# A two-layer diffusion step on one core: raw weights of late pairs loaded a pair ahead, ten early pairs, prompts' products a pair later

## The chip, the cores and the metric

The kernel runs on one core of a Trainium2 chip. Its engines are TensorE (PE, the matrix products), VectorE (DVE), ScalarE (ACT), GpSimd (POOL) and SyncE (SP), which only issues transfers; ACT and POOL issue some too. Each works through its own list of instructions in order. The metric is the device time of one execution in microseconds (us), the median of the runs shown.

## The reference

Two layers work on a prompt of 128 tokens and a sample of 1024 tokens, with the same weights. In each layer a normalised and modulated input is multiplied by one wide matrix; its columns feed three branches (a gated convolution, attention and multi-scale pooling) and the gates by which the branches are merged:

```python
    hn = rms_norm(x, g_pre) * (1 + scale) + shift
    proj = hn @ w_in
    (a_b, a_c, a_x, a_z, q_down, kv_down, b_z, c_u, c_z, merge_logits) = jnp.split(proj, split_points, axis=-1)
    y_a = jax.nn.silu(a_z) * (a_b * centred_conv3(a_c * a_x, conv_w, conv_b))
    ...
    y_b = jax.nn.silu(b_z) * attn
    y_c = jax.nn.silu(c_z) * multiscale_pool(c_u, pool_w, pool_scale)
    branches = jnp.einsum('bsnc,ncd->bsnd', jnp.stack([y_a, y_b, y_c], axis=2), w_branch)
    merged = jnp.sum(gates * branches, axis=2)
    out = rms_norm(merged @ w_o, g_post)
    return x + gate * out, own_latent
```

## The kernel before

**Products.** All values are float32. Each operand of a large product is split into a high part (a cast to float32r) and a low part (what is left), and a product is the sum of three matmuls, high by high, low by high and high by low (`mm3`, line 107). The cast is mostly ACT's (`a_copy`, line 68), the subtraction DVE's (`sub`, line 88). A matrix for the sample has its feature index across the partitions and 1024 tokens, in two halves of 512.

**Pairs.** The product with `w_in` is done in 29 pairs of output blocks (class `Pair`), each for the whole sample by a scheme with seven products instead of eight; a product is four `mm3`, so 12 matmuls of 128x512. They have the names 11, 21, T2, T1, T3, 22 and T4 by the part of the input that they use. The prompt's product with the same columns is 24 matmuls of 128x256. The first two products and the prompt's need only half of the input's preparation. So nine pairs (`EARLY`) run twice: as "early" pairs at the start of a layer (11, 21 and the prompt's, in `early`), before the whole input is ready, with the result of 11 stored in `d_p1`; and as "late" pairs at the end (the other five products, in `run`). The other 20 (`ORDER`) are "full" pairs and run between them.

**Preparation.** `Pair.prep` is a generator, whose first step loads the raw weights (1 MB a pair, as two tiles), and whose later steps form sums and differences (POOL, DVE), casts (ACT) and subtractions (DVE). `ahead` pulls the generators of the next pairs one step at a time after each product; so what lies where in each engine's list follows from these pulls. `tick` does the same for background work such as `conv_gen`, `s_pool` (the sample's pooling, line 1068 loads its input), `p_pool` (the prompt's pooling, transposes at line 1108), the modulation's products and, at the start of a layer, the normalisation of the prompt (`hnp_gen`) and of the input's second half (`gB`), which ends in `t_gen`, the sums over the input that the later products use.

**Buffers and queues.** 44 slots of 128x1040 (`S()`, tiles named s) are given out in turn; an operation that writes a new slot waits until the one handed out 44 earlier is no longer read. `put` (lines 125 and 130) has a store issued by SP some steps later. SP issues in order, so a store that waits for its data holds the loads behind it.

**After the pairs.** `mid_phase` starts `p_pool`, runs `merge` for branch 0 and for branch 2 (the second adds to what the first left: a product by the gate on DVE, an addition on POOL and a store issued by POOL, line 984), and `produce` makes the attention's operands. It begins with POOL's memsets of `q32` (line 1301) and of `qa` (line 1313), into which ACT then copies. Weights of these stages are split by `pump`, two of three casts on POOL (`p_copy`, line 82). After attention, `last_merge` and `out_phase` end the layer; the latter's `first` and the generators `gP` (prompt) and `gB` carry the start of the next layer.

Of the kernel before, what the change touches and what calls it, by code (L numbers as in the profile page):

```python
# [26 lines left out]
EARLY = (0, 1, 2, 3, 4, 5, 6, 7, 25)  # L27
# [6 lines left out]
def hybrid_step_kernel(ctx: ExitStack, tc: tile.TileContext, I, O):  # L34
# [32 lines left out]
    def a_copy(out, in_):  # L67
        act.copy(out=out, in_=in_)  # L68
# [128 lines left out]
    lead = [6]  # L197
    freed = [0]
# [371 lines left out]
    class Pair:  # L570
        def __init__(self, l, p, kind):
            self.l, self.p, self.kind = l, p, kind
            self.gen = self.prep()

        def prep(self):
            raw = [S(), S()]
            g, h = SOURCE[self.p]
            for i in range(2):
                if g == 14:
                    sp.dma_start(out=raw[i][:, 0:1024], in_=I["w_in2"][self.l, i])  # L580
                    continue
                for t in range(2):
                    src = I["w_in"][self.l, g, 2 * i + t].rearrange("p (k c)->p k c", k=2)
                    sp.dma_start(out=raw[i][:, 512 * t:512 * t + 512].rearrange("p (k c)->p k c", k=2),
                                 in_=src[:, :, 256 * h:256 * h + 256])
# [31 lines left out]
            if not late_:  # L617
                low(raw[0], w[0])
            if early_:
# [64 lines left out]
    def early(l, units, epis, mid, pend):  # L684

        gP, gB = pend
        for us in [units[0:3]] + [[u] for u in units[3:]]:
            first, steps = len(us) > 1, 2 if us[0] in units[-2:] else 1
            p1 = []
            for u in us:  # L690
                ready(u)
                h = H()
                a_copy(h, u.prod(u.w[0], 0, "11"))
                act.dma_start(out=d_p1[EARLY.index(u.p)], in_=h)
                p1.append(h)
                if mid:
                    next(mid, None)
                ahead(None, 3 - steps, steps)
                if not first or u is us[1]:
                    tick()  # L700
            for u, h in zip(us, p1):
                v = H()
                add(v, u.prod(u.w[1], 0, "21"), h)
                epis[u.p][0](0, 0, v)
                ahead(None, 3 - steps, steps)
                if not first or u is not us[1]:
                    tick()
            finish(gP)
            for u in us:
                epis[u.p][1](u.prompt())  # L710
                ahead(None, 3 - steps, steps)
                tick()
            mid = None
# [135 lines left out]
    ORDER = list(range(8, 16)) + list(range(19, 23)) + [16, 17, 18, 23, 24, 26, 27, 28]  # L849
# [6 lines left out]
    def in_phase(l, e, mid, pend):  # L856
# [8 lines left out]
        ya, yp = [], S(F32R)  # L865
# [29 lines left out]
        return ya, yp  # L895
# [64 lines left out]
    def merge(l, n, y, yp, first, hooks=()):  # L960
# [15 lines left out]
        def out(ps):  # L976
# [11 lines left out]
        for g in range(2):  # L988
# [5 lines left out]
            for m in range(4):  # L994
                out(prod_m(B, m, y_get(y), 0))
# [12 lines left out]
            for m in range(4):  # L1008
                out(prod_m(B, m, y_get(y), 1))
# [245 lines left out]
    def mid_phase(l, ya, ypa):  # L1255
# [4 lines left out]
        yc, ypc = [], S(F32R)  # L1260
        gp = spawn(p_pool(l, ypc))
# [19 lines left out]
    def produce(l, R):  # L1281
# [16 lines left out]
        A["q32"] = q32  # L1298
        for h in range(8):
# [11 lines left out]
        qa = S()  # L1311
        A["qa"] = qa
        pool.memset(qa[:, 0:1024], 0.0)
# [504 lines left out]
    def out_phase(l, mg, pt):  # L1818
# [54 lines left out]
    with tc.manual_schedule():  # L1873
# [21 lines left out]
        next(units[0].gen)  # L1895
        load_mod(1)
        load_mod(3)
        next(units[1].gen)
        next(units[2].gen)
# [23 lines left out]
        def mid():  # L1923
# [6 lines left out]
            hn_first(0, 0, xt[0], (2, 3))  # L1930
            next(gP)
# [16 lines left out]
        for kp in range(4):  # L1948
            for j in range(2):
                x = xt[0][kp][:, 512 * j:512 * j + 512]  # L1950
                mul(x, x, r, eng=dve if kp < 2 else pool)
# [3 lines left out]
        hn_first(0, 0, xt[0], (0, 1))  # L1955
        gP, gB = spawn(hnp_gen(0, xp)), spawn(first_b())
# [3 lines left out]
        for l in range(L):  # L1960
            R = mid_phase(l, *in_phase(l, units, then if l else mid(), pend))
            A = produce(l, R)
            yb = attention(l, R, A)
            finish(gmod)
# [117 lines left out]
```

## Time and profile before

| | before |
|---|---|
| runs | 2825.68, 2824.93, 2816.12 us; median 2824.93 |
| profiled execution | 2818.2 us by its own time, span 2816.4 us |
| PE busy | 2587.5 us (92%) |
| DVE, ACT, POOL busy | 1806.8, 1078.9, 879.0 us |
| moved by DMA | 371.01 MB, mean 132 GB/s |

The span is what the profiler saw between the first and the last instruction; the own time of the execution is a little longer. A busy share is a mean over stages with different limits, so the stages are looked at apart: layer 0 has its early pairs up to about 170 us, full pairs to 600, late pairs to 770, merges to 943, `produce` to about 983 and attention to 1280; layer 1 has its early pairs from 1446 to 1570, late pairs from 1980 to 2168, merges to 2301 and `produce` to about 2340.

### The profile page before, as it was taken

The page shows a single profiled execution, that of the slowest core. Times are in us where ns is not written, and L with a number is a line of the kernel's source. Part 1 is how long each engine was busy: PE and PEld are TensorE (multiplying, and loading weights), DVE is VectorE, ACT ScalarE, POOL GpSimd, SP SyncE. Part 2 cuts the span into 40 slices and gives each one's busy share as a digit, 9 for nine tenths or more (in the row PEclk, how much of TensorE's full clock was granted, in tenths as well). Part 3 has the DMA queues.
Part 4 walks back from the last instruction along what each step waited for, and adds up shares of the span by engine and source line. Part 5 has one row for each costly group of instructions (what it writes and reads, how often), then busy time and mean ns, then how long its engine had stood idle before and what let it go on. Part 6 is the DMA issues. An engine that isn't in the chain of part 4 may idle for free. (4 is left out here: it accounts for less than half of the span.)

```text
span 2816.4 us, 32523 instructions
## 1 busy us (share of the span) xinstructions
PE 2587.5 (92%) x11672; PEld 2051.2 (73%) x11672; DVE 1806.8 (64%) x2434; ACT 1078.9 (38%) x1752; POOL 879.0 (31%) x772
## 2 busy tenths in 40 slices
PE   4899999999899889899977999999988898998997
PEld 2777777777677767677866888888766677776785
DVE  4845555657747578886577444666675657888655
ACT  4532222332322257774345222323322214776621
POOL 2322211102122646754032222111211174566402
PEclk7899999999999999999998999999999999999999
DMA  7333345546497400005254222444447751000433
GB/s 276 110 125 97 97 154 176 189 149 191 159 321 246 153 5 8 23 23 180 90 182 158 84 71 83 154 146 164 164 146 273 252 201 27 5 8 31 124 112 112
DMA packets 213506, 371.01 MB, mean 132 GB/s; under 512 B 20576, under 2 KB 105568, under 8 KB 213344
## 3 DMA queue, kind: packets, MB, share of 16 engines
q1 hardware_dynamic: 170896, 275.32, 30.2%
q10 hardware_dynamic: 31680, 56.38, 5.4%
q0 software_dynamic: 10768, 37.23, 3.5%
q8 instruction: 92, 1.51, 0.2%
q14 instruction: 70, 0.57, 0.1%
HBM read 254.45 MB, written 112.23 MB: 130 GB/s over the span
## 5 line engine op out<-in xcount | busy, mean ns | idle before, releaser
L107 PE MATMUL p<-s,s 128*128 128x512 f32 (+3 forms) x10876 | 2464.8, 386 | 142.1 <-ACT s L68 47.2
L107 PEld LDWEIGHTS p<-s,s 128*128 128x128 f32 (+1 forms) x10876 | 1953.9, 191 | 625.9 <-DVE s L88 55.6
L88 DVE TENSOR_TENSOR s<-s,s 128x1024 fp32r<-128x1024 f32 (+7 forms) x565 | 628.3, 1125 | 317.2 <-ACT s L68 106.9
L68 ACT CAST s<-s 128x1024 fp32r<-128x1024 f32 (+3 forms) x341 | 333.4, 998 | 554.0 <-DVE s L88 319.4
L88 DVE TENSOR_TENSOR h<-p,h 128x512 f32<-128x512 f32 (+1 forms) x480 | 317.0, 661 | 333.8 <-PE p L107 239.2
L88 POOL TENSOR_TENSOR s<-s,s 128x512 f32<-128x512 f32 (+2 forms) x109 | 215.7, 1982 | 857.1 <-DMA s<-in_w_in_dram 625.3
L88 DVE TENSOR_TENSOR s<-h,s 128x512 fp32r<-128x512 f32 (+4 forms) x316 | 302.7, 970 | 129.2 <-ACT s L79 64.8
L79 ACT ACTIVATE h<-p 128x512 f32<-128x512 f32 (+2 forms) x364 | 208.5, 573 | 227.2 <-PE p L107 214.9
L79 ACT ACTIVATE h<-h 128x512 f32<-128x512 f32 (+1 forms) x196 | 123.0, 629 | 315.4 <-DVE h L88 260.9
L88 POOL TENSOR_TENSOR h<-h,h 128x512 f32<-128x512 f32 (+2 forms) x72 | 98.1, 1362 | 302.5 <-DVE h L88 173.7
L79 ACT ACTIVATE s<-p 128x512 fp32r<-128x512 f32 x288 | 174.1, 604 | 2.4 <-POOL h L88 2.4
L88 DVE TENSOR_TENSOR h<-h,h 128x512 f32<-128x512 f32 (+3 forms) x122 | 90.9, 745 | 95.6 <-ACT h L79 93.0
L1536 DVE TENSOR_REDUCE c<-p 128x1 f32<-128x448 f32 x256 | 147.9, 611 | 6.6 <-PE p L107 6.5
L82 POOL TENSOR_SCALAR s<-s 128x1024 fp32r<-128x1024 f32 (+2 forms) x65 | 79.4, 1227 | 208.8 <-DMA s<-in_w_o_dram 64.8
L88 POOL TENSOR_TENSOR s<-s 128x512 f32<-128x512 f32 x94 | 132.3, 1407 | 29.6 <-DVE s L88 27.1
L68 ACT COPY h<-p 128x512 f32<-128x512 f32 (+2 forms) x108 | 51.6, 478 | 217.6 <-PE p L107 207.6
L88 POOL TENSOR_TENSOR s<-h,s 128x512 fp32r<-128x512 f32 x64 | 89.0, 1391 | 126.5 <-ACT s L79 125.1
L68 ACT CAST s<-h 128x512 fp32r<-128x512 f32 (+5 forms) x92 | 47.8, 524 | 164.0 <-DVE h L88 99.0
L68 ACT COPY s<-p 64x512 f32<-64x512 f32 (+3 forms) x116 | 64.2, 566 | 112.1 <-PE p L107 75.2
L88 DVE TENSOR_TENSOR s<-p,s 128x512 f32<-128x512 f32 (+2 forms) x118 | 72.6, 631 | 47.6 <-PE p L107 31.4
L88 POOL TENSOR_TENSOR s<-s,h 128x512 f32<-128x512 f32 x26 | 40.8, 1574 | 116.6 <-DVE h L100 76.1
L107 PE MATMUL p<-s,h 128*128 128x512 f32 (+1 forms) x184 | 57.2, 421 | 15.1 <-ACT s L68 13.2
(122 smaller groups left out, 944.9 us busy)
## 6 DMA issues: line engine op xcount, KB each, us to landing
s<-in_w_in_dram SPq DMA_DIRECT2D x296, 256.0 KB, 4.2
s<-in_w_mod_dram SPq DMA_DIRECT2D x48, 512.0 KB, 4.9
d_gate<-h ACTq DMA_DIRECT2D x96, 256.0 KB, 4.6
s<-d_gate SPq DMA_DIRECT2D x64, 256.0 KB, 5.6
s<-in_w_br_dram SPq DMA_DIRECT2D x24, 512.0 KB, 4.7
s<-in_xT_dram SPq DMA_DIRECT2D x16, 512.0 KB, 6.3
s<-d_ya POOLq DMA_DIRECT2D x16, 512.0 KB, 10.7
s<-d_yc POOLq DMA_DIRECT2D x16, 512.0 KB, 10.6
```

Source lines behind the costliest of these rows:

```text
L68: act.copy(out=out, in_=in_)
L79: act.activation(out=out, in_=in_, func=func, scale=scale, bias=bias)
L82: pool.tensor_scalar(out=out, in0=in_, scalar1=1.0, scalar2=0.0, op0=ALU.mult, op1=ALU.add)
L88: eng.tensor_tensor(out=out, in0=in0, in1=in1, op=op)
L107: pe.matmul(out=out, lhsT=lhsT, rhs=rhs, start=start, stop=stop)
L1536: dve.reduce_max(out=mv[:, i, qt:qt + 1], in_=ps[:, 0:448], axis=AX.X)
```

## The change

- `EARLY` has a tenth pair, 26, which leaves `ORDER`.
- The loads of a pair's raw weights become `load(i)`. An early pair loads its second half only after the cast of the first. In `in_phase` the loads of the next two late pairs are issued before the present pair runs. At the start of layer 0 the first halves of four pairs are loaded between the modulation's weights, the second halves after them.
- `early` takes four pairs (layer 0) or three (layer 1) together: first all their products 11, with only the first half of each pair's weights ready, then all their products 21, then 11 and 21 of the next pair, and only then the prompt's products of all of them.
- `p_pool` is started three pairs before the end of `in_phase` in place of the start of `mid_phase`.
- In `merge`, the additions of the second half of the sample (c = 1) go from POOL to DVE and their stores from POOL to SP. `pump` has ACT do the casts outside of attention. `produce` clears `qa` before `q32`.
- At the boundary of the layers the loads of `gB` start later in layer 0, and `gB` goes ahead of `gP`. At the start the products of the third and fourth input tiles with the row norm, on POOL, come after the first half of the normalisation.

```diff
-EARLY = (0, 1, 2, 3, 4, 5, 6, 7, 25)
+EARLY = (0, 1, 2, 3, 4, 5, 6, 7, 25, 26)
...
-            if i % 3 == 1:
+            if i % 3 == 1 or not att[0]:
                 a_copy(hi[:, 0:n_], st[:, 0:n_])
...
+        def first(self):
+
+            while not self.w0:
+                next(self.gen)
 
         def prep(self):
...
+            self.load(0)
+            if self.kind != "early":
+                self.load(1)
+            raw = self.raw
             yield
...
             if early_:
+                self.load(1)
+                yield
                 w[1] = high(raw[1])
...
+        us = units[:nb]
+        us[0].first()
+        for i, u in enumerate(us):
+            p1(u)
+            if i + 1 < nb:
+                us[i + 1].first()
+            keep1(u)
+            next(mid, None)
+            step()
+        for _ in mid:
+            pass
+        for i, u in enumerate(us):
+            ready(u)
+            if i == 0:
+                ready(us[1])
+            p2(u)
+            ahead(None, 1) if i else None
+            tick()
+        finish(gP)
+        for i, u in enumerate(units[nb:]):
+            steps = 2 if u in units[-2:] else 1
+            ready(u)
+            p1(u)
+            ahead(None, 3 - steps, steps)
+            keep1(u)
+            tick()
+            p2(u)
+            ahead(None, 3 - steps, steps)
+            tick()
+            for x in (us if i == 0 else []) + [u]:
+                epis[x.p][1](x.prompt())
                 ahead(None, 3 - steps, steps)
                 tick()
...
+            if u[min(i + 1, len(u) - 1)].kind == "late":
+                for y in u[i + 1:i + 3]:
+                    y.load(0), y.load(1)
+            if i == len(u) - 3:
+                ypc.append(S(F32R))
+                gp.append(spawn(p_pool(l, ypc[0])))
             run(l, x, epis[x.p], None if last else u[i + 1], hooks)
...
-            if first:
+            if not first:
+                add(x, x, t[:, 512:1024], eng=None if c else pool)
+            if first or c:
                 put(dst, x)
             else:
-                add(x, x, t[:, 512:1024], eng=pool)
                 pool.dma_start(out=dst, in_=x)
...
+        qa = S()
+        A["qa"] = qa
+        pool.memset(qa[:, 0:1024], 0.0)
         for h in range(8):
             z0 = 32 if h % 2 else 96
             pool.memset(q32[h][z0:z0 + 32, 0:1024], 0.0)
...
         finish(gA)
         gB = post_chunk(l, 1, B, True)
-        next(gB)
+        if l + 1 == L:
+            next(gB)
...
-                next(gP), next(gB)
-                yield
-                next(gP), next(gB)
+                next(gB), next(gP)
+                yield
+                next(gB), next(gP)
                 spawn(gB), spawn(gP)
```

The first place is SP's list among layer 1's late pairs, before: `d_p_88` is `d_p1`, in_w_in the raw weights (two tiles a pair), `d_yc` a store of the sample's pooling.

```order
540 L647 DMA h_15912<-d_p_88 128x512
541 L584 DMA s_15928<-in_w_in_dram 128x2x256 x2
542 L584 DMA s_15929<-in_w_in_dram 128x2x256 x2
543 L125 DMA d_yc<-h_15897 128x512
544 L130 DMA d_yc<-h_15964 128x512
545 L1068 DMA s_16025<-d_u 128x2x512
546 L647 DMA h_16045<-d_p_88 128x512
547 L584 DMA s_16061<-in_w_in_dram 128x2x256 x2
548 L584 DMA s_16062<-in_w_in_dram 128x2x256 x2
```

The same place of the same list after the change:

```order
551 L665 DMA h_15817<-d_p_88 128x512
552 L1129 DMA h_15920<-d_z 128x512
553 L1129 DMA h_15922<-d_z 128x512
554 L588 DMA s_15940<-in_w_in_dram 128x2x256 x2
555 L588 DMA s_15943<-in_w_in_dram 128x2x256 x2
556 L665 DMA h_15946<-d_p_88 128x512
557 L130 DMA d_yc<-h_15991 128x512
558 L130 DMA d_yc<-h_16044 128x512
559 L1114 DMA s_16067<-d_u 128x2x512
560 L588 DMA s_16071<-in_w_in_dram 128x2x256 x2
561 L588 DMA s_16074<-in_w_in_dram 128x2x256 x2
562 L665 DMA h_16077<-d_p_88 128x512
```

Before, the load of `d_p1` for the next pair stands ahead of raw weights that are loaded while that pair's predecessor runs; after, the raw weights of a pair stand one load of `d_p1` earlier than the pair that uses them, so those behind the store at 558 belong to a pair later.

The second place is POOL's list where the second merge of layer 0 ends and `produce` begins, before:

```order
184 L88 TENSOR_TENSOR s_6841<-s_6841 128x512
185 L984 DMA d_part<-s_6841 128x512
186 L88 TENSOR_TENSOR s_6860<-s_6860 128x512
187 L984 DMA d_part<-s_6860 128x512
188 L88 TENSOR_TENSOR s_6879<-s_6879 128x512
189 L984 DMA d_part<-s_6879 128x512
190 L88 TENSOR_TENSOR s_6914<-s_6914 128x512
191 L984 DMA d_part<-s_6914 128x512
192 L82 TENSOR_SCALAR s_6973<-s_6965 128x1024
193 L1301 MEMSET s_6981 32x1024
...
200 L1301 MEMSET s_6988 32x1024
201 L1313 MEMSET s_7043 128x1024
```

After, in the same list:

```order
165 L88 TENSOR_TENSOR s_6833<-s_6833 128x512
166 L1030 DMA d_part<-s_6833 128x512
167 L88 TENSOR_TENSOR s_6814<-s_6814 128x512
168 L1052 DMA d_partp<-s_6814 128x512
169 L1346 MEMSET s_7002 128x1024
170 L1349 MEMSET s_6994 32x1024
...
177 L1349 MEMSET s_7001 32x1024
178 L88 TENSOR_TENSOR s_7082<-s_7012,s_6990 128x1024
```

Of the eight equal memsets the first and the last are shown. The four additions with their stores and the cast of a weight have left this list, and `qa` (128x1024) is cleared ahead of the eight tiles of `q32`.

The third place is DVE's list in layer 1's early pairs, before: lines with 128x1024 on s tiles are subtractions that give low parts (`s_11438` and `s_11474`, the second halves of the weights of the second and third pair), `h_11509` and `h_11521` the prompt's normalised rows.

```order
1214 L88 TENSOR_TENSOR h_11455<-p_11456,h_11342 128x512
1215 L88 TENSOR_TENSOR s_11438<-s_11414,s_11437 128x1024
1216 L88 TENSOR_TENSOR h_11476<-p_11477,h_11377 128x512
1217 L88 TENSOR_TENSOR s_11474<-s_11415,s_11473 128x1024
1218 L88 TENSOR_TENSOR h_11500<-s_11440 128x512
1219 L103 TENSOR_SCALAR h_11509<-p_11504,cols_0_101 128x128 x4
1220 L88 TENSOR_TENSOR s_11503<-h_11509,s_11502 128x512
1221 L103 TENSOR_SCALAR h_11521<-p_11516,cols_0_101 128x128 x4
1222 L88 TENSOR_TENSOR s_11503<-h_11521,s_11502 128x512
```

After, in the same list (`s_11458` is the low part of the third pair's second half, and `h_11502` the result of that pair's product 21):

```order
1223 L103 TENSOR_SCALAR h_11482<-p_11477,cols_0_101 128x128 x4
1224 L88 TENSOR_TENSOR s_11476<-h_11482,s_11475 128x512
1225 L103 TENSOR_SCALAR h_11494<-p_11489,cols_0_101 128x128 x4
1226 L88 TENSOR_TENSOR s_11476<-h_11494,s_11475 128x512
1227 L88 TENSOR_TENSOR s_11458<-s_11363,s_11457 128x1024
1228 L88 TENSOR_TENSOR h_11502<-p_11503,h_11397 128x512
1229 L88 TENSOR_TENSOR h_11522<-s_11460 128x512
```

The third pair's low part has moved from ahead of the prompt's rows to behind them.

## Rows read from the trace of the kernel before

**Rows 1.** The page's first part: busy time, share and instructions by engine.

```profile
PE 2587.5 (92%) x11672; PEld 2051.2 (73%) x11672; DVE 1806.8 (64%) x2434; ACT 1078.9 (38%) x1752; POOL 879.0 (31%) x772
```

**Rows 2.** Stretches: length, busy time (instructions) by engine, granted clock, DMA share, GB/s.

```profile
170.00:600.00 430.00, 429.13 (x2048) 336.76 (x2047) 241.24 (x299) 117.73 (x152) 83.35 (x70) 1.00 0.43 140
600.00:770.00 170.00, 154.74 (x665) 117.33 (x664) 115.98 (x169) 52.65 (x77) 27.25 (x22) 0.96 0.53 168
770.00:943.00 173.00, 160.97 (x666) 127.59 (x665) 109.05 (x180) 36.94 (x57) 52.67 (x65) 0.95 0.81 284
943.00:983.00 40.00, 32.08 (x144) 25.14 (x143) 17.09 (x30) 10.06 (x29) 26.11 (x27) 0.91 0.25 73
...
1446.00:1570.00 124.00, 94.11 (x479) 78.76 (x478) 86.22 (x86) 59.02 (x80) 39.84 (x28) 0.86 0.48 161
...
1980.00:2168.00 188.00, 171.81 (x724) 137.27 (x723) 129.89 (x177) 58.94 (x85) 37.83 (x41) 0.95 0.54 179
2168.00:2301.00 133.00, 117.94 (x494) 93.46 (x493) 83.85 (x150) 26.62 (x42) 42.27 (x46) 0.95 0.79 277
2301.00:2340.00 39.00, 33.75 (x148) 25.51 (x147) 19.46 (x33) 10.83 (x32) 24.35 (x25) 0.91 0.24 68
```

**Rows 3.** PE's waits from 600 to 770: releaser, us, times, longest.

```profile
PE p L107 <- DMA s<-in_w_mod_dram: 5.8, 2, 5.0
PE p L107 <- ACT h L68: 4.4, 1, 4.4
```

**Rows 4.** PE's waits from 1980 to 2168.

```profile
PE p L107 <- ACT s L68: 8.6, 2, 8.4
...
PE p L107 <- DVE h L88: 2.5, 1, 2.5
```

**Rows 5.** PE's waits from 805 to 943.

```profile
PE p L107 <- DVE s L100: 4.0, 1, 4.0
...
PE p L1108 <- DMA s<-d_uzp: 2.7, 1, 2.7
PE p L107 <- ACT s L68: 2.3, 1, 2.3
```

**Rows 6.** PE's waits from 2168 to 2301.

```profile
PE p L1108 <- DMA s<-d_uzp: 6.4, 1, 6.4
PE p L107 <- DVE s L100: 5.3, 1, 5.3
PE p L107 <- ACT s L68: 2.5, 1, 2.5
```

**Rows 7.** DVE's timeline in both layers' late pairs; brackets: idle before, releaser.

```profile
727.86 2.49 DVE L88 TENSOR_TENSOR s<-s,s 128x512 f32<-128x512 f32 x2 [10.50 <-DMA s<-in_w_in_dram]
...
2087.10 2.48 DVE L88 TENSOR_TENSOR s<-s,s 128x512 f32<-128x512 f32 x2 [9.95 <-DMA s<-in_w_in_dram]
```

**Rows 8.** SP's waits from 1980 to 2168 (line 130 stores d_yc).

```profile
SPq L130 <- DVE h L88: 15.4, 2, 10.3
```

**Rows 9.** POOL's timeline at the end of layer 0's second merge.

```profile
949.91 1.30 POOL L88 TENSOR_TENSOR s<-s 128x512 f32<-128x512 f32 x1
951.50 0.56 POOL L984 DMA_DIRECT2D d_part<-s  x1 [0.30 <-POOL s L88]
...
953.21 7.86 POOL L1301 MEMSET s<- 32x1024 f32 x8
```

**Rows 10.** ACT's timeline at the start of layer 0's operands.

```profile
962.12 1.93 ACT L68 COPY s<-p 128x128 f32<-128x128 f32 x6 [17.55 <-POOL s L1313]
```

**Rows 11.** DVE's timeline in layer 1's early pairs, subtraction alone and sum beside POOL.

```profile
1495.76 1.22 DVE L88 TENSOR_TENSOR s<-s,s 128x1024 fp32r<-128x1024 f32 x1
...
1508.55 3.42 DVE L88 TENSOR_TENSOR s<-s,s 128x1024 f32<-128x1024 f32 x1 [0.51 <-POOL s L103]
```

**Rows 12.** PE's timeline in layer 1's early pairs.

```profile
1457.83 0.80 PE L107 MATMUL p<-s,s 128*128 128x512 f32 x1 [7.85 <-ACT s L68]
...
1483.79 5.34 PE L107 MATMUL p<-s,s 128*128 128x256 f32 x24 [10.23 <-ACT s L68]
```

More of the change, by code (lines that the diff above doesn't have):

```diff
@@ L197, in hybrid_step_kernel @@
     lead = [6]
+    att = [False]
     freed = [0]
@@ L573, in __init__, with load @@
             self.gen = self.prep()
-        def prep(self):
[L576 to L585, printed above, removed]
+            self.raw = [None, None]
+            self.w0 = False
+        def load(self, i):
+            if self.raw[i] is not None:
+                return
+            self.raw[i] = r = S()
+            g, h = SOURCE[self.p]
+            if g == 14:
+                sp.dma_start(out=r[:, 0:1024], in_=I["w_in2"][self.l, i])
+                return
+            for t in range(2):
+                src = I["w_in"][self.l, g, 2 * i + t].rearrange("p (k c)->p k c", k=2)
+                sp.dma_start(out=r[:, 512 * t:512 * t + 512].rearrange("p (k c)->p k c", k=2),
+                             in_=src[:, :, 256 * h:256 * h + 256])
+        def first(self):
+            while not self.w0:
+                next(self.gen)
+        def prep(self):
+            self.load(0)
+            if self.kind != "early":
+                self.load(1)
+            raw = self.raw
             yield
@@ L686, in early, with p1, keep1, p2 @@
         gP, gB = pend
[L687 to L710, printed above, removed]
+        nb = 4 if l == 0 else 3
+        def p1(u):
+            u.ps1 = u.prod(u.w[0], 0, "11")
+        def keep1(u):
+            u.h1 = H()
+            a_copy(u.h1, u.ps1)
+            act.dma_start(out=d_p1[EARLY.index(u.p)], in_=u.h1)
+        def p2(u):
+            v = H()
+            add(v, u.prod(u.w[1], 0, "21"), u.h1)
+            epis[u.p][0](0, 0, v)
+        us = units[:nb]
[29 more added lines that the diff above has]
+                epis[x.p][1](x.prompt())
                 ahead(None, 3 - steps, steps)
                 tick()
-            mid = None
     def run(l, u, epi, nxt=None, hooks=()):
@@ L847, in hybrid_step_kernel @@
     SOURCE += [(12, 1), (13, 0), (13, 1), (14, 0)]
-    ORDER = list(range(8, 16)) + list(range(19, 23)) + [16, 17, 18, 23, 24, 26, 27, 28]
+    ORDER = list(range(8, 16)) + list(range(19, 23)) + [16, 17, 18, 23, 24, 27, 28]
     def units_of(l):
@@ L864, in in_phase @@
         flush()
-        ya, yp = [], S(F32R)
+        ya, yp, ypc, gp = [], S(F32R), [], []
         def load_ya(m):
@@ L894, in in_phase @@
         finish(g2)
-        return ya, yp
+        return ya, yp, ypc[0], gp[0]
     def conv_gen(l):
@@ L974, in fetch, with out @@
             got.append((t, d_part[4 * g + m, c]))
-        def out(ps):
+        def out(ps, c):
             t, dst = got.popleft()
@@ L994, in merge @@
             for m in range(4):
-                out(prod_m(B, m, y_get(y), 0))
+                out(prod_m(B, m, y_get(y), 0), 0)
                 if hooks:
@@ L1008, in merge @@
             for m in range(4):
-                out(prod_m(B, m, y_get(y), 1))
+                out(prod_m(B, m, y_get(y), 1), 1)
                 if hooks:
@@ L1253, in kvq_post, with mid_phase @@
         return R
-    def mid_phase(l, ya, ypa):
+    def mid_phase(l, ya, ypa, ypc, gp):
         lead[0] = 4
@@ L1259, in mid_phase @@
         R = kvq_post(l)
-        yc, ypc = [], S(F32R)
-        gp = spawn(p_pool(l, ypc))
+        yc = []
         def load_yc(m):
@@ L1894, in hybrid_step_kernel @@
         units = units_of(0)
-        next(units[0].gen)
+        for u in units[:4]:
+            u.load(0)
         load_mod(1)
         load_mod(3)
-        next(units[1].gen)
-        next(units[2].gen)
+        for u in units[:4]:
+            u.load(1)
         xp = S()
@@ L1947, in hybrid_step_kernel, with times_r @@
         r = rstd(bsum(norm_x(0)), DM)
[L1948 to L1951, printed above, removed]
+        def times_r(kps, eng):
+            for kp in kps:
+                for j in range(2):
+                    x = xt[0][kp][:, 512 * j:512 * j + 512]
+                    mul(x, x, r, eng=eng)
+        times_r((0, 1), dve)
         x_new()
@@ L1962, in hybrid_step_kernel @@
             A = produce(l, R)
+            att[0] = True
             yb = attention(l, R, A)
+            att[0] = False
             finish(gmod)
```

5 lines of the change are left out of this document (2 added, 3 removed).

## The prediction

> **What bounds the kernel now.** The page comes first: TensorE (PE) is busy for 2587.5 of 2816.4 us [rows 1], so whatever the other engines save counts only where PE stands still for them. The next view is the table of stretches, which shows where that is. In the full pairs of layer 0 PE is busy 429.13 of 430 us at a granted clock of 1.00; in the late pairs, in the merges, in the first part of the attention's operands and at the start of layer 1 it is idle and its clock falls below 1.00 [rows 2]. The clock has two levels, 1.2 and 2.4 GHz, so a mean of 0.95 over 133 us means that 13.3 us ran at the lower level, which costs up to 133 x 0.05 = 6.65 us on top of the idle time. The third view, PE's waits in a stretch, names what came last before each wait [rows 3 to 6]; the timeline of another engine, or its own waits, then show why that work was late [rows 7 to 12]. The change touches each of those places, and nothing in the attention or in the full pairs, where I take no difference.
>
> **The change part by part.** TensorE's work stays the same: 10 + 19 pairs in place of 9 + 20, and a pair split into early and late still has seven products and one for the prompt. The tenth early pair costs 1 MB of loads, one cast and one subtraction more per layer; all lie in stretches in which DMA's share is about half and ScalarE's (ACT's) busy time 52.65 of 170 us [rows 2], so I cost them at nothing. If that cover were gone, they would cost their own time, some 3 us a layer.
>
> *Raw weights a pair ahead.* In both layers VectorE (DVE) sits idle for about 10 us in the late pairs, waiting for in_w_in [rows 7]. SyncE issues its transfers in order, and a store of d_yc that waits for DVE holds it, once for 10.3 us [rows 8]; the weights stand behind that store. What is then late on DVE is late on ACT and in the end on PE: a wait of 4.4 us in layer 0 [rows 3], of 8.4 and 2.5 us in layer 1 [rows 4]. In the order after, the two loads of the pair after next stand ahead of such a store. I take these waits as gone. The wait of 5.0 us for the modulation weights in layer 0 stays: their load is not moved. Of the clock's cost, 170 x 0.04 = 6.8 and 188 x 0.05 = 9.4 us, I give back 1.6 and 2.1, since other waits lie in the same stretches. That makes -6 in layer 0 (between 0 and -4.4 - 5.8 - 6.8 = -17) and -13 in layer 1 (between 0 and -8.6 - 2.5 - 9.4 = -20.5).
>
> *The prompt's pooling earlier.* Its load of d_uzp, its transposes and its small additions now start three pairs before the end of the late pairs in place of the start of the first merge. PE waits for exactly these three things: d_uzp, ACT's cast ahead of the pool_w product, and DVE's L100 ahead of the second merge's prompt product. That is 2.7 + 2.3 + 4.0 = 9.0 us in layer 0 [rows 5] and 6.4 + 2.5 + 5.3 = 14.2 us in layer 1 [rows 6]. With 3 us of each stretch's clock cost (173 x 0.05 = 8.65 and 133 x 0.05 = 6.65) I get -12 and -17, between 0 and -17.6, and 0 and -20.9. The work itself does not vanish: some 10 us of small DVE operations move into late pairs, where DVE is busy 129.89 of 188 us [rows 2]; PE's eight transposes are in its queue there and can wait for the same load. I charge a quarter of the 23.2 us for that: +6 (between 0 and +23).
>
> *GpSimd relieved.* At the end of the second merge GpSimd (POOL) does an addition (1.30 us) and a DMA issue (0.56 us) per product, one every 2.18 us, and begins the 7.86 us of memsets only at 953.21 [rows 9]. ACT's copies into qa wait for the memset behind these, idle for 17.55 us until 962.12 [rows 10], and PE waits 7.9 us for ACT. After, the last four additions are DVE's and their stores SyncE's (4 x 2.18 = 8.7 us off POOL), the casts of weights are ACT's, and qa's memset stands ahead of the others, which is 7.86 us more. Together 16.6 us, more than the 7.9 us waited, so the wait can go entirely; next late are the products with the cosines, still behind the eight memsets. I take -9 in layer 0 (idle 40 - 32.08 = 7.9 and 40 x 0.09 = 3.6 of clock, so between 0 and -11.5), -5 in layer 1 (39 - 33.75 = 5.25 and 3.5, between 0 and -8.8). The eight additions a layer on DVE last some 0.7 us each and lie beside 109.05 busy of 173 us, so they cost nothing; without that cover they would cost 5.5 us.
>
> *Early pairs.* Layer 1: PE waits 10.23 us for ACT's cast of the prompt's normalised rows [rows 12]. The new order has only five products ahead of that chain where there were six (third unit's second product now needs a subtraction that stands behind the chain in DVE's queue), but the wait for the third unit's cast behind GpSimd's work, 7.85 us [rows 12], mostly goes. One product is 12 x 429.13 / 2048 = 2.5 us by [rows 2]. A further subtraction, for the fifth unit, falls into the sums that DVE and POOL make beside each other, where one of 128x1024 took 3.42 us in place of 1.22 [rows 11]. I take +6, between -8 and +15: two such waits of 5 to 6 us, less half the 7.85. Layer 0: the first normalisation loses POOL's company, but lows of the second to fourth units fall behind the other half of it; I take 0, and for the bounds the longest wait of [rows 12] either way: -10 and +10.
>
> On those sums the Trainium skill has a rule (SBUF — State Buffer, "SBUF: two separate sides"): VectorE with two SBUF inputs and GpSimd take turns at a shared pair of ports, and of the one that comes second it says "the other fully blocks". By it a subtraction of 1.22 us would take as long as the rest of a GpSimd addition and its own time; 3.42 us agrees with that only in kind. It speaks against the new place of GpSimd's products with the row norm at the start, which now run beside DVE's subtractions; by it the start would come out at the end of its range, and the time at 2782 us.
>
> **The sum.** -6 - 13 - 12 - 17 + 6 - 9 - 5 + 6 + 0 = -50 us. The profiled execution took 2818.2 us by its own time (span 2816.4), so 2768; the runs shown have a median of 2824.9, 6.7 us above it, and one lies below it, so I add half of that: **2772 us**.
>
> **The rivals.**
>
> *The raw weights are late all the same.* They only change places in SyncE's queue; a load a pair ahead needs its slot a pair earlier, and in layer 0 the modulation weights and two d_yc stores still stand between two such loads. SyncE was held 15.4 us in two waits by one store line in layer 1 [rows 8]. For it: DMA waits move easily. Against: a late pair has five products, 5 x 2.5 = 12.5 us, more than the 10.5 us that DVE waits. The 19 us are lost and the time is 2772 + 19 = 2791. Chance 0.14.
>
> *The early pairs lose more.* If the third unit's second product, the fourth's first and the fifth's each wait as long as the longest wait there now (10.23 us), less the one that there is, it is 20 us more: 2792. For it speaks that DVE's order puts the subtraction behind the whole chain; against, that PE is idle there already. Chance 0.10.
>
> *GpSimd is not what holds the operands.* The copies into qa find another wait, such as ACT's own casts of weights in front of them, and the 14 us stay: 2786. Chance 0.06.
>
> *Slower: the ring of slots turns against it.* Slots are handed out in turn, 44 of them, and each waits until the one handed out 44 before is free. Raw weights loaded a pair ahead hold two slots a pair longer, and the tenth early pair takes four slots more. If from then on every late pair's preparation waited for a slot, PE would wait in each of 20 late pairs; at the 10 us of [rows 7] at most, at 4 us likely, that is +80 - 50 = +30 against the profile, 2850. It decides from 50 / 20 = 2.5 us per late pair. Against: the pair whose tiles lie 44 back is done when the loads are issued. Chance 0.08.
>
> **How the numbers follow.** The forecast above has a chance of 0.62, with a range of its own from 2750 to 2788. The rivals hold 0.14, 0.10, 0.06 and 0.08. The range that holds 8 in 10 leaves out the slot case and the best sums of all bounds: 2748 to 2808. A measurement of this kernel tells some 0.5% from no change, 14 us: below 2811 counts as faster. The forecast, most of the first two rivals and the third lie there, 0.84; half of the slot case and what is left of the others lie within, 0.09; the rest is slower, 0.07.
>
> **What the profile after would show.** DVE's two idle times for in_w_in in the late pairs are gone, and so are PE's waits for d_uzp and for L100 in the merges; the transposes for it lie in the late pairs. ACT's wait for the memset of qa is short, and POOL's busy time is lower by the 16 additions of 1.30 us (21 us) and by the casts. The stretch from 1446 has one wait of 10 us ahead of the third unit's second product. The clock of the merges is 0.98 or more. I am wrong if the late pairs still show waits for in_w_in, if PE waits for the slots' loads in several late pairs, or if the two starts of layers together take over 20 us more than now.

## The result and the profile after

The changed kernel takes 2779.57 us (median of 4 runs, 2774.80 to 2783.02), the kernel before beside it 2820.84 us. The ratio is 0.9852 (95% interval 0.9825 to 0.9880), 1.5% faster: 41 us, where 50 against the profile and 53 against the first median were forecast, with 2772 us and a range from 2748 to 2808.

The page after, first lines (busy time, share, instructions; the granted clock in 40 slices):

```profile
span 2773.0 us, 32545 instructions
...
PE 2569.7 (93%) x11672; PEld 2037.3 (73%) x11672; DVE 1812.7 (65%) x2452; ACT 1103.0 (40%) x1779; POOL 820.1 (30%) x715
...
PEclk8799999999999999999987999999999999999999
```

TensorE (PE) has as many instructions as in [rows 1], GpSimd (POOL) 57 fewer and 59 us less to do, ScalarE (ACT) 24 us more. The table of stretches after, cut at nearly the same places of the program as [rows 2], with one difference: layer 0's late pairs end, and its merges begin, at 805 here. In the trace before that place is 810, so 40 us of [rows 2]'s stretch from 770 to 943 are still late pairs.

```profile
185.00:615.00 430.00, 429.12 (x2049) 336.82 (x2048) 241.35 (x300) 117.59 (x152) 81.84 (x70) 1.00 0.43 140
615.00:805.00 190.00, 182.64 (x795) 141.50 (x794) 139.25 (x209) 62.40 (x92) 36.36 (x42) 0.98 0.65 216
805.00:930.00 125.00, 118.54 (x511) 94.01 (x510) 89.09 (x145) 32.17 (x49) 35.72 (x37) 0.99 0.85 300
930.00:960.00 30.00, 29.96 (x139) 23.22 (x137) 17.32 (x32) 11.89 (x34) 12.21 (x13) 1.00 0.27 72
1421.00:1571.00 150.00, 108.92 (x525) 88.04 (x524) 91.83 (x89) 62.78 (x85) 39.38 (x28) 0.84 0.44 148
...
1980.00:2151.00 171.00, 160.91 (x685) 129.04 (x684) 128.32 (x189) 59.28 (x86) 34.59 (x40) 0.97 0.57 191
2151.00:2270.00 119.00, 111.84 (x478) 88.36 (x477) 86.03 (x143) 28.62 (x41) 29.62 (x30) 0.99 0.84 295
2270.00:2306.00 36.00, 36.00 (x170) 28.48 (x168) 19.17 (x35) 15.22 (x40) 18.21 (x19) 1.00 0.39 124
```

The trace before, cut there too:

```profile
600.00:810.00 210.00, 194.74 (x838) 149.84 (x837) 140.09 (x197) 63.01 (x91) 40.85 (x44) 0.97 0.58 191
810.00:943.00 133.00, 120.97 (x493) 95.08 (x492) 84.94 (x151) 26.58 (x42) 39.07 (x44) 0.94 0.80 283
```

The merges' clock rises from 0.94 and 0.95 to 0.99, and `produce` has no idle time left on PE in its first 30 us. The start of layer 1 went the other way: 150 - 108.92 = 41 us idle and a clock of 0.84, where [rows 2] had 30 us and 0.86.

To split the 42 us by stage I read when the same matmul (by its number on PE) starts in each trace, and take the differences. The tenth early pair moves 24 matmuls of 128x512 and 24 of 128x256 a layer from the end to the start; I count them as 8.4 us (the kernel with that pair alone is 8.2 and 8.8 us longer there). Worked out from PE's records, us, after minus before:

```
stage                              difference   without the move   forecast
start and early pairs, layer 0        +14.2           +5.8             0
late pairs, layer 0                   -23.2          -14.8            -3
merges and operands, layer 0          -18.6          -18.6           -21
boundary and early pairs, layer 1     +26.1          +17.7            +6
late pairs, layer 1                   -20.0          -11.6           -10
merges and operands, layer 1          -17.6          -17.6           -22
full pairs, attention, the rest        -2.9           -2.9             0
sum                                   -42.0          -42.0           -50
```

(The forecast's +6 for the pooling's work in the late pairs is split between the two. Of the -2.9 in the parts for which nothing was forecast, about -6 lies in layer 1's attention and +3 in the others; the last section shows how much such a part varies.) PE's waits in the merges of layer 1, after (releaser, us in total, times, longest):

```profile
PE p L107 <- DVE s L88: 5.1, 3, 3.5
PE p L107 <- DMA s<-d_ya: 1.9, 1, 1.9
```

Of the three waits of [rows 6], 14.2 us, none is left. In the boundary the picture is another; PE's timeline after, the start of layer 1:

```profile
1427.96 5.85 PE L107 MATMUL p<-s,s 128*128 128x512 f32 x24 [1.46 <-DVE s L88]
1438.93 4.68 PE L107 MATMUL p<-s,s 128*128 128x512 f32 x11 [5.13 <-DVE s L88]
...
1448.02 0.80 PE L107 MATMUL p<-s,s 128*128 128x512 f32 x1 [2.74 <-ACT s L68]
1460.28 4.31 PE L107 MATMUL p<-s,s 128*128 128x512 f32 x11 [11.47 <-DVE s L88]
...
1498.51 8.61 PE L107 MATMUL p<-s,s 128*128 128x512 f32 x36 [6.67 <-DVE s L88]
```

and VectorE (DVE) in the same time:

```profile
1453.70 1.36 DVE L103 TENSOR_SCALAR h<-p,cols 128x128 f32<-128x128 f32 x4
1455.75 0.69 DVE L88 TENSOR_TENSOR s<-h,s 128x512 fp32r<-128x512 f32 x1 [0.69 <-ACT s L68]
1456.36 1.36 DVE L103 TENSOR_SCALAR h<-p,cols 128x128 f32<-128x128 f32 x4
1458.40 0.69 DVE L88 TENSOR_TENSOR s<-h,s 128x512 fp32r<-128x512 f32 x1 [0.68 <-ACT s L68]
1459.01 1.22 DVE L88 TENSOR_TENSOR s<-s,s 128x1024 fp32r<-128x1024 f32 x1
```

The prompt's rows end at 1459.09, the third pair's subtraction follows to 1460.23, and at 1460.28 PE goes on: the 11.47 us are the wait of [rows 12] (10.23), now ahead of the third pair's second product. The 7.85 us of [rows 12] are gone, but 5.13 us have come for the second pair's subtraction, and 6.67 us are waited for subtractions behind the sums of DVE and POOL.

### The profile page after: what moved, and what is told of

Its sections match the earlier page's. It is cut to its first block, busy times and chain, and to the rows that moved or that the text cites. A ratio compares the mean times of both kernels' runs of the same rounds, so it can differ in the third digit from the quotient of the medians.

```text
span 2773.0 us, 32545 instructions
## 1 busy us (share of the span) xinstructions
PE 2569.7 (93%) x11672; PEld 2037.3 (73%) x11672; DVE 1812.7 (65%) x2452; ACT 1103.0 (40%) x1779; POOL 820.1 (30%) x715
## 5 line engine op out<-in xcount | busy, mean ns | idle before, releaser
L88 DVE TENSOR_TENSOR s<-s,s 128x1024 fp32r<-128x1024 f32 (+6 forms) x567 | 620.1, 1105 | 261.6 <-ACT s L68 142.9
L68 ACT CAST s<-s 128x1024 fp32r<-128x1024 f32 (+4 forms) x368 | 358.6, 997 | 540.1 <-DVE s L88 263.7
L68 ACT COPY h<-p 128x512 f32<-128x512 f32 (+1 forms) x108 | 51.6, 478 | 220.0 <-PE p L107 205.7
L88 POOL TENSOR_TENSOR s<-s 128x512 f32<-128x512 f32 x78 | 113.0, 1449 | 44.2 <-DVE s L88 43.9
L82 POOL TENSOR_SCALAR s<-s 128x1024 fp32r<-128x1024 f32 (+1 forms) x40 | 52.3, 1313 | 93.2 <-ACT s L68 55.7
L107 PE MATMUL p<-s,h 128*128 128x512 f32 (+1 forms) x184 | 54.6, 409 | 17.4 <-ACT s L68 16.0
```

The costliest lines, as they stand in the source:

```text
L82: pool.tensor_scalar(out=out, in0=in_, scalar1=1.0, scalar2=0.0, op0=ALU.mult, op1=ALU.add)
L88: eng.tensor_tensor(out=out, in0=in0, in1=in1, op=op)
L107: pe.matmul(out=out, lhsT=lhsT, rhs=rhs, start=start, stop=stop)
```

## The experiments

Each kernel was timed in three rounds beside the kernel before.

**The order of the starts alone**, on the kernel before:

```diff
-        for us in [units[0:3]] + [[u] for u in units[3:]]:
...
+        us = units[:nb]
+        us[0].first()
...
+            self.load(0)
+            if self.kind != "early":
+                self.load(1)
...
+                next(gB), next(gP)
...
+        times_r((2, 3), pool)
```

Pairs' count, late pairs' loads, pooling, merge and operands stay as before.

> The kernel before with the new order of the two layers' starts alone (nine early pairs, no earlier loads for late pairs, pooling, merge and operands as before). Theory 1, the new order of the early pairs costs by itself what the two traces differ there (5.9 us in layer 0, 17.6 us in layer 1): 23 us slower than the kernel before, some 2844 us. Theory 2, the order is neutral and the loss comes from the tenth early pair or from what else the change puts beside it: within 6 us of the kernel before.

2833.89 us against 2821.56; ratio 1.0040 (1.0025 to 1.0055), 12 us slower. By the same matmuls 4.8 us lie in layer 0 and 16.1 at the boundary; the attention of layer 1, which is the same, was 6.5 us shorter in that trace. The sign is theory 1's; by these stages the amount is 21 of its 23 us, by the rounds about half of it.

**The old order of the starts**, in the changed kernel:

```diff
-        us = units[:nb]
-        us[0].first()
...
+        for us in [units[0:3]] + [[u] for u in units[3:]]:
...
-        times_r((2, 3), pool)
```

The load of an early pair, the boundary and the start of layer 0 are as before too; the ten pairs stay.

> The changed kernel with the order of both starts as before, ten early pairs and all else kept. Theory 1: the 23 us come back, some 2757 us, and PE's wait of 11.5 us ahead of the third pair's second product in layer 1 is gone. Theory 2: the loss stays, within 6 us of 2780.

2759.96 us, ratio 0.9780 (0.9766 to 0.9795). Some 20 of the 23 us come back, so the new order itself costs what the traces differ there. Theory 2 falls.

**The old order in layer 1 alone:**

```diff
+    def early(l, *a):
+        (early_new if l == 0 else early_old)(l, *a)
```

At the boundary `gP` goes ahead of `gB` again, and the loads of `gB` start as early as before.

> The changed kernel with the order as before in layer 1 alone (early pairs in layer 1 and the end of layer 0). Theory 1: the 17.6 us of layer 1 come back, some 2762 us, and layer 0 stays as it is. Theory 2: within 6 us of 2780.

2769.01 us, ratio 0.9812 (0.9788 to 0.9836), 11 us less than the changed kernel. The boundary is 10.2 us shorter, not 17.6: `early_old`, the order before, ran there with the split load of an early pair, whose second half comes a step later. With the load in one piece, as in the experiment above, boundary and early pairs were 8.8 us longer than in the kernel before, 0.4 us beyond the 8.4 that move.

**The first pairs' weights made ready before their second products:**

```diff
             if i == 0:
-                ready(us[1])
+                for y in us[1:]:
+                    ready(y)
```

> The changed kernel with the weights of all first pairs made ready before the first of the second products, so that the third pair's subtraction stands ahead of the prompt's rows in DVE's list. Theory 1a, that subtraction's place is the cost in layer 1: the wait of 11.5 us shrinks by the length of one product, 3 to 6 us, and the time falls by as much, some 2775. Theory 1b, the prompt's chain is what everything waits for: the wait moves to the prompt's products and the time stays within 3 us. In layer 0, where four pairs run together, preparing all of them ahead can cost: up to 10 us.

2761.07 us, ratio 0.9786 (0.9770 to 0.9802): 18.5 us less than the changed kernel by two lines. In layer 0 the first full pair begins 14.2 us earlier (161.1 against 175.3 us), where I expected a loss. In layer 1 only 3.9 us come of it. PE's timeline of this kernel, layer 0 and then layer 1:

```profile
75.46 6.14 PE L107 MATMUL p<-s,s 128*128 128x512 f32 x24
87.25 0.80 PE L107 MATMUL p<-s,s 128*128 128x512 f32 x1 [5.64 <-ACT s L68]
...
1427.67 3.03 PE L107 MATMUL p<-s,s 128*128 128x512 f32 x12
1446.98 0.80 PE L107 MATMUL p<-s,s 128*128 128x512 f32 x1 [16.28 <-ACT s L68]
```

In layer 0 two second products run without a wait; in the changed kernel the same two waited for subtractions behind the prompt's rows and behind the normalisation:

```profile
76.90 0.51 PE L107 MATMUL p<-s,s 128*128 128x512 f32 x1 [1.15 <-ACT s L68]
86.04 5.06 PE L107 MATMUL p<-s,s 128*128 128x512 f32 x11 [8.63 <-DVE s L88]
93.99 0.50 PE L107 MATMUL p<-s,s 128*128 128x512 f32 x1 [2.89 <-ACT s L68]
95.67 5.06 PE L107 MATMUL p<-s,s 128*128 128x512 f32 x11 [1.17 <-DVE s L88]
```

In layer 1 the third pair's second product runs too, and then PE waits 16.28 us for the cast of the fourth pair's weights, behind the same chain. So theory 1a holds in layer 0, and 1b describes layer 1: there are fewer products ahead of the chain than the chain is long.

**Late pairs' loads a pair ahead, alone:**

```diff
+            if u[min(i + 1, len(u) - 1)].kind == "late":
+                for y in u[i + 1:i + 3]:
+                    y.load(0), y.load(1)
```

> The kernel before with the late pairs' raw weights loaded a pair ahead, and nothing else of the change. Theory 1 (the prediction's step): DVE's two idle times of 10 us for in_w_in go and with them PE's waits of 4.4, 8.4 and 2.5 us and part of the low clock: 6 us in layer 0 and 13 in layer 1, some 2802 us. Theory 2, these waits have another cause (the stores that hold SyncE, the pooling's own chain): under 5 us, and the wait of 8.4 us for ACT's cast ahead of the pooling's product stays.

2806.67 us, ratio 0.9948 (0.9932 to 0.9965), 15 us. But the waits did not go. The late pairs became 5.5 and 3.8 us shorter, PE's waits of 4.4 and 8.4 us of [rows 3, 4] are still there with 4.2 and 6.8 us, and DVE's idle time of [rows 7] has only another name. PE's waits in layer 1's late pairs, then SyncE's (SP) timeline there, POOL's and DVE's:

```profile
PE p L107 <- ACT s L68: 7.3, 2, 6.8
```

```profile
2055.55 0.33 SPq L125 DMA_DIRECT2D d_yc<-h  x1
2066.28 0.32 SPq L130 DMA_DIRECT2D d_yc<-h  x1
2066.77 0.37 SPq L1086 DMA_DIRECT2D s<-d_u  x1
2067.23 2.80 SPq L588 DMA_DIRECT2D s<-in_w_in_dram  x4
```

```profile
2076.77 1.30 POOL L88 TENSOR_TENSOR s<-s,s 128x512 f32<-128x512 f32 x1 [28.45 <-DMA s<-in_w_in_dram]
```

```profile
2078.11 2.51 DVE L88 TENSOR_TENSOR s<-s,s 128x512 f32<-128x512 f32 x2 [9.87 <-POOL s L88]
```

SP still stands at a store of d_yc until 2066.28 and issues the weights behind it. POOL's sum comes before DVE's; once its weights are as late as DVE's, DVE's wait is put down to POOL. Theory 2 by its place, though not by its amount: 9.3 of the 15 us lie in the late pairs, and most of the rest in the attention, which this kernel does not touch.

**The same, with the store out of the way.** `s_pool` calls `flush` ahead of its load of d_u, and that brings the store just put into SP's list to the front:

```diff
+            while held:
+                put(*held.pop(0))
...
-                put(d_yc[1, gi][:, a], f(yl))
+                if gi < 3:
+                    held.append((d_yc[1, gi][:, a], f(yl)))
+                else:
+                    put(d_yc[1, gi][:, a], f(yl))
```

> The kernel with the late pairs' loads a pair ahead alone, and beside that the pooling's stores of d_yc put behind its next load of d_u, so that they no longer stand ahead of the late pairs' weights in SyncE's list when their data is late. Theory 1, the store that waits for DVE is what holds the weights: GpSimd's and DVE's waits of about 10 us for them go, and with them PE's waits of 4 to 7 us behind: 8 to 15 us less than the loads a pair ahead alone (2807), some 2795. Theory 2, the loads wait for slots that PE still reads: SyncE is held at the loads in place of the store, and the time stays within 4 us of 2807.

2785.79 us, ratio 0.9868 (0.9853 to 0.9882): 21 us less than the loads alone, more than theory 1 said. SP's timeline at the same place:

```profile
2040.96 0.38 SPq L1087 DMA_DIRECT2D s<-d_u  x1
2041.43 8.73 SPq L588 DMA_DIRECT2D s<-in_w_in_dram  x4
...
2054.96 4.34 SPq L125 DMA_DIRECT2D d_yc<-h  x2
```

The store now follows the weights. DVE's wait of 9.87 us is gone, the late pairs are 12.5 and 9.8 us shorter than with the loads alone, and PE's longest wait in those of layer 1 is 4.2 in place of 6.8 us. In layer 0 PE's wait for the modulation's weights, 4.6 us with the loads alone, is gone as well: they stood behind the same store.

**The prompt's pooling earlier, alone:**

```diff
+            if i == len(u) - 3:
+                ypc.append(S(F32R))
+                gp.append(spawn(p_pool(l, ypc[0])))
```

> The kernel before with the prompt's pooling started three pairs before the end of the late pairs, and nothing else of the change. Theory 1 (the prediction's step): the three waits of each layer's merges go, 12 and 17 us, less some 6 for what it does to the late pairs: 23 us faster, some 2798 us. Theory 2, the work takes its waits along into the late pairs: the late pairs lose 10 us or more, and the gain is under 12 us.

2800.50 us, ratio 0.9926 (0.9912 to 0.9941), 21.5 us. The late pairs lose nothing (they are 2.3 and 2.4 us shorter), and of the waits for d_uzp, the cast and L100 none is seen. Theory 1 by place, and the time is within 2 us of its amount. By stage it is not: merges and operands became 7.2 and 6.3 us shorter, where 12 and 17 were forecast. Other waits stand there now; in layer 1's merges the one for d_ya is 4.9 us, where it was 0.8:

```profile
PE p L107 <- DMA s<-d_ya: 4.9, 3, 2.1
```

**GpSimd's relief alone**, and **only `qa` cleared first:**

```diff
-            if i % 3 == 1:
+            if i % 3 == 1 or not att[0]:
...
+                add(x, x, t[:, 512:1024], eng=None if c else pool)
...
+        pool.memset(qa[:, 0:1024], 0.0)
         for h in range(8):
```

and of this the memset alone, without the casts and the additions:

```diff
+        pool.memset(qa[:, 0:1024], 0.0)
         for h in range(8):
```

> The kernel before with GpSimd's relief alone (half of the second merge's additions and stores and the casts of weights taken from it, qa cleared first). Theory 1 (the prediction's step): the waits of 7.9 and 4.5 us at the start of the operands go, 9 and 5 us, some 2807 us. Theory 2, ACT's casts or the memsets of q32 hold the operands instead: under 5 us, and PE waits there for ACT or POOL as long as before.

> The kernel before with qa cleared ahead of q32 alone. Theory 1, the eight memsets ahead of it (7.86 us) are the wait: PE's 7.9 us in layer 0 goes, and in layer 1 part of the 4.5, so that most of the 27 us of GpSimd's whole relief is seen, at least 10. Theory 2, GpSimd's additions in front of the memsets hold it as well: PE still waits 1 to 3 us in layer 0, nothing changes in layer 1, and the gain is 5 to 10 us.

The relief gave 2794.94 us, ratio 0.9906 (0.9892 to 0.9921): 27 us, twice what was forecast. The memset alone gave 2817.59 us, ratio 0.9982 (0.9972 to 0.9993): 5 to 6 us. Its layer 0, ACT, POOL and PE:

```profile
956.17 1.93 ACT L68 COPY s<-p 128x128 f32<-128x128 f32 x6 [8.84 <-POOL s L1316]
```

```profile
956.19 7.89 POOL L1319 MEMSET s<- 32x1024 f32 x8
964.17 4.64 POOL L88 TENSOR_TENSOR s<-s,s 128x1024 f32<-128x1024 f32 x2
```

```profile
970.01 5.21 PE L107 MATMUL p<-s,s 128*128 128x512 f32 x14 [6.31 <-DVE h L88]
```

ACT comes in time, and PE waits 6.31 us for the products with the cosines, behind the eight memsets. That is what the prediction named as next late. So the change takes additions and casts off POOL as well; the two were not tried apart. In the changed kernel POOL's last addition ahead of the memsets is that of the prompt's product, the four behind it are DVE's, and ACT no longer waits for qa:

```profile
924.18 0.97 POOL L1346 MEMSET s<- 128x1024 f32 x1
925.22 7.85 POOL L1349 MEMSET s<- 32x1024 f32 x8
```

```profile
925.87 1.05 ACT L68 CAST s<-s 128x1024 fp32r<-128x1024 f32 x1 [14.04 <-DMA s<-in_w_ukk_dram]
```

By the same matmuls the relief shortens merges and operands by 7.8 and 7.3 us and the late pairs by some 2 each; most of the rest of the 27 (5.4 us) lies in layer 1's attention, which this kernel does not touch and which varies from kernel to kernel (last section).

**The tenth early pair alone:**

```diff
+EARLY = (0, 1, 2, 3, 4, 5, 6, 7, 25, 26)
```

> The kernel before with the tenth early pair alone, in the old order of the starts. Theory 1, the pair only moves work from the full pairs to the two ends: within 5 us of the kernel before (the three other parts alone gave 15, 22 and 27 us, together 64, and the changed kernel with the old starts gave 62). Theory 2, it moves the late pairs against the pooling's stores and brings them a gain of their own: the late pairs 4 to 5 us a layer shorter beyond the 8.4 us of products moved, some 2814.

2803.39 us, ratio 0.9930 (0.9913 to 0.9946), 20 us, which the prediction held for nothing. Without the 8.4 us that move, the late pairs are 8.7 and 5.1 us shorter. DVE's waits for POOL there are 9.1 us in four (layer 0) and 8.2 us in two (layer 1), where [rows 7] had one of 10 in each. One full pair less stands between the pooling's last loads and the first late pair, so stores and late pairs meet elsewhere. That is theory 2 by its place, with more than its amount; that the stores are the reason is argued, not shown, and where the rest of the 20 us lies is open.

**The two best starts together**, then **without the store**:

```diff
+                for y in us[1:]:
+                    ready(y)
...
+    def early(l, *a):
+        (early_new if l == 0 else early_old)(l, *a)
...
+            if self.kind != "early" or self.l:
+                self.load(1)
```

The first two lines are in `early_new`; in layer 1 an early pair's load is in one piece, and the boundary's order is the one before.

> The changed kernel with, in layer 0, the weights of the first four pairs made ready before their second products, and in layer 1 the order of the start as before. The runs so far give, against the changed kernel, 14 us less in layer 0 and 16 less in layer 1. If the two are independent: 2750 us. If the gain in layer 0 came from what layer 1 does: 2760.

> The fastest kernel so far (2748 us) with the pooling's stores of d_yc behind its next load of d_u. Theory 1, the store is what is left of the late weights' lateness: PE's waits of 6.4 and 8.8 us in the late pairs shrink and the time falls by 5 to 12 us, some 2740. Theory 2, with ten early pairs the weights no longer wait for the store: within 4 us of 2748.

2747.59 us, ratio 0.9735 (0.9720 to 0.9749): the two gains add up. With the stores behind the load of d_u as above, 2742.76 us, ratio 0.9716 (0.9701 to 0.9730). The 5 us are at theory 1's lower edge and lie where they should: the late pairs of layer 1 take 195.3 us in place of 200.9, those of layer 0 the same within 1 us. But PE's two long waits did not shrink as theory 1 says; they are 7.9 and 8.2 us. This version beats both kernels, by 81 us the one before.

## Why the prediction was right, and where it was not

The sum came out 8 us from the measured time, with terms mis-sized and one mechanism wrong. That is in part luck, since the errors had opposite signs. By the table of stages the early pairs cost 17.5 us more than forecast and the merges and operands gave 6.8 us less; the late pairs gave 13.4 us more, and 2.9 us came from parts for which nothing was forecast.

*Pooling earlier*: right in its place. The three waits of each layer went, and alone it gave 21.5 us against the 23 of the sum. But the merges and operands gave 13.5 us of the 29 forecast there, since other waits came up behind those that went, and the charge of 6 us for its work in the late pairs was not needed: they became 4.7 us shorter.

*GpSimd relieved*: right in its chain and near in size: merges and operands gave 7.8 and 7.3 us, where 9 and 5 were forecast. The cover of 16.6 us was not one sum, though. The memset's new place (7.86 us) brings only ACT's copies forward; the products with the cosines stand behind the eight memsets either way, and with the memset alone PE waited 6.31 us for them. It took the rest of the relief to end that.

*Raw weights a pair ahead*: the step that failed is "in the order after, the two loads of the pair after next stand ahead of such a store. I take these waits as gone". Loads of a later pair do, but those that DVE and POOL then need were still behind it; SP issued them at 2067.23, right after the store that it had waited with until 2066.28. The first rival (weights late all the same) is what happened to this part when it stood alone: 3.8 of the 13 us in layer 1. That SP was held by the store and not by a slot was shown by moving the store. The Trainium skill (DMA: Bandwidth & Descriptors, "Anatomy of one DMA — SWDGE (gpsimd) path") says of DMA engines that they do not wait on semaphores, and that "any semaphore wait happens on the issuing sequencer before dispatch"; for SP's store the trace agrees, with 10.3 us of SP's waiting ahead of the store's issue [rows 8].

The same hold is in the changed kernel, and with it the first of the prediction's signs of being wrong (late pairs that still wait for in_w_in), under POOL's name. Layer 1's late pairs after, SP, POOL and DVE:

```profile
2059.30 2.36 SPq L130 DMA_DIRECT2D d_yc<-h  x2
...
2062.26 2.61 SPq L588 DMA_DIRECT2D s<-in_w_in_dram  x4
```

```profile
2069.30 1.31 POOL L88 TENSOR_TENSOR s<-s,s 128x512 f32<-128x512 f32 x1 [16.39 <-DMA s<-in_w_in_dram]
```

```profile
2070.64 2.50 DVE L88 TENSOR_TENSOR s<-s,s 128x512 f32<-128x512 f32 x2 [5.43 <-POOL s L88]
```

SP waited there 20.0 us with the store. PE did not wait meanwhile: it ran without a gap for 44.61 us from 2055.96 on.

*The late pairs' time in the changed kernel* came out better than forecast in layer 0 (-14.8 against -3) all the same. The largest part of that is the tenth pair's, costed at nothing: alone it gave 8.7 us there. The four parts alone gave 15 (loads), 20 (tenth pair), 21.5 (pooling) and 27 us (relief), together 84, but the changed kernel with the old starts gave 62. In the late pairs their gains overlap: added up they are 18.6 and 13 us, in that kernel 15.1 and 10.8. That is 6 of the 22 us; where the others lie is open. The waits of 6.5 and 6.8 us that the changed kernel has in the late pairs, for the cast ahead of the pooling's product, stay open; with the stores out of the way they were still 7.9 and 8.2 us.

*Early pairs*: the term for layer 1 was mis-sized, +6 against +17.7, past its bound of +15. The wait of 10.23 us stayed, moved by one product as said; but PE's idle time rose from 29.9 to 41.1 us and the time lost to the clock from at most 124 x 0.14 = 17.4 to at most 150 x 0.16 = 24 us, together 17.8: the first of these was counted with 6, the second not at all. In layer 0, 0 against +5.8. Second rival in its place, at 12 of its 20 us. Together the two starts took 23.5 us more, past the 20 that the prediction named as a sign of being wrong. For layer 0 the fix shows the reason: `ready` of a pair puts its cast and subtraction into ACT's and DVE's lists at that point, and everything that `tick` had put there before (prompt's rows, normalisation) comes first. In layer 1 it gave only 3.9 us back, and the old order 17; the order of the early products and that of `gB` and `gP` were not tried apart there. The time by the rule on the shared ports, 2782 us, is nearer to the measured one than the forecast is, but its reason, a loss of 10 us in layer 0 to contention, is not what happened: with GpSimd's products in the same place, the same work in another order gave 14 us back.

*Third and fourth rival*: no sign of the third, POOL held the operands. Of the fourth there is a sign, but no cost is seen: SP's loads of weights wait for PE to free slots, in layer 1's late pairs 20.0 us where it was 14.1, and no wait of PE's there is put down to a load:

```profile
SPq L588 <- PE p L107: 20.0, 5, 7.1
```

## What to carry to other kernels

A store that waits for its data holds every load behind it on the same queue; look first at what stands ahead of a late load, then at how early it was put there. Where lists are made by pulling generators, a product's operands should be put into the lists before any long chain that the product doesn't need, as the two lines of `ready` show (18.5 us, 14.2 of them in layer 0). When a wait's releaser changes its name and the wait keeps its length, the cause is further up.

## What the runs showed of the hardware

On DVE a subtraction of 128x1024 took 1.22 us alone and a sum of that shape 3.42 us beside one on POOL [rows 11]. POOL's sum alone is seen at the start of layer 0's operands in the trace before, POOL and then DVE:

```profile
962.06 4.73 POOL L88 TENSOR_TENSOR s<-s,s 128x1024 f32<-128x1024 f32 x2
```

```profile
964.49 2.85 DVE L88 TENSOR_TENSOR s<-s,h 128x512 f32<-128x512 f32 x1 [9.47 <-POOL s L88]
...
967.97 0.69 DVE L88 TENSOR_TENSOR s<-s,h 128x512 f32<-128x512 f32 x1
```

DVE is idle until 964.49, so the first of POOL's two sums ran alone, in about 4.73 / 2 = 2.4 us. 1.22 + 2.4 = 3.6, close to 3.42, so the two take turns in amount as well, nearer to the rule that the prediction quoted than it said. DVE's own operation beside POOL's second sum took 2.85 us; the same one took 0.69 us later, while POOL cleared a tile.

The attention and the last merge of a layer, which no experiment touched, took between 285.1 and 293.8 us in layer 1 from trace to trace (from the same two matmuls), with the same instructions on PE, DVE, ACT and POOL. A part that is alone in a comparison of single profiles is therefore known to some 5 us at best, and the timed rounds decide.
